# One PSUM ring for scores and transposed weights, and a third bank kept for the matmuls of the MLP, in a hybrid attention layer on one core

## The chip, the cores and the metric

The kernel runs on one core of one Trainium2 chip. The metric is the device time of one launch in microseconds, as the median of several runs. A profile of one execution comes with it: what each engine did and when, and what ended each stretch in which it was idle.

## What is computed

One step of a streaming encoder layer over 2048 prompt tokens and 32 sample tokens, with 1024 channels, all in fp32. The part of the reference that matters here is the long-range ("A") attention, with two softmax maps per head:

```python
def diff_core(q, k, v, bias, mask, lam):
    s = jnp.einsum('bqhmd,bkhmd->bhmqk', q, k).astype(jnp.float32) * (HEAD_DIM ** -0.5) + bias[:, None]
    s = jnp.where(mask, s, NEG)
    p = jax.nn.softmax(s, axis=-1)
    w = p[:, :, 0] - lam * p[:, :, 1]
    return jnp.einsum('bhqk,bkhe->bqhe', w.astype(v.dtype), v)
```

There are 4 such heads, and 8 heads of a short-range ("B") attention that sees the 64-token chunk and the 8 chunks before it. Both are fed by one input projection. Their outputs are normed, concatenated and projected (`w_out`), and added to the input. A squared-ReLU MLP with 4096 hidden channels, a gate (`w_ple_gate`, `w_ple_proj`) and a last norm follow.

## The kernel before

**Arithmetic.** Every fp32 operand of a matmul is split into a high and a low fp32r part. A product is three matmuls (`mm3`, lines 212 to 218): high by high, high by low, low by high. Line numbers 216, 217 and 218 therefore stand for the matmuls of every projection; the tile's name tells which: `ops` output projection, `ups` and `dps` the MLP's two halves, `gps` and `pps` the gate.

**Blocks.** Tokens come in four blocks of 512 (the last one with the 32 sample tokens). The A attention works on pairs of 128-query tiles, 256 queries, numbered j = 0 to 7; j = 8 stands for the sample. `JA0` (pairs 0 to 3) runs early; `JA1 = [(4, 5), (6, 7, 8)]` is the second long-range part. For each list of `JA1` the loop runs over the 4 heads, and in each head over the pairs of the list: 8 pairs, then 12, of which 4 are samples.

**One pair** (`attn_a_pair`, from line 597 on). For each of its two query tiles and each of the two maps, up to four score tiles `s` of 128 x 512 are computed (line 639, two matmuls each) and moved by VectorE to `e`, with the row maximum taken on the way (line 646; line 648 where the bias `ba` is added, which happens in the last block only). ScalarE takes the exponential of the whole row (654), and ScalarE and VectorE combine the two maps into weights (659, 660). `e` has two buffers for each map, one for each query tile, so a pair can't empty its first scores before the weights of the pair before it have been transposed. Then, for each 512 keys and each query tile, TensorE transposes the weights four to a tile `tpp` (698), ScalarE and VectorE read it as `pH` (705) and `pL` (706), and three matmuls per 128 keys add into `o` (712 to 714), which ScalarE moves to `os` (716). The bias tile `ba` of a head has one buffer, `q` has two.

**PSUM.** There are eight banks of 128 x 512 fp32. Up to and through the projection of the last two blocks they are: `mm` 2 and `mmx` 1 (projections, MLP; a `Rings` object hands them out as mm, mm, mmx in turn), `pss` 2 (scores), `pst` 2 (transposes), `pso` 1. Before the second long-range part the kernel closes `mmx`, so that output projection and MLP have the two banks of `mm`, and opens its bank as `psy`: scores then take turns in three banks (s, s, y) and transposes in their own two. After the MLP of blocks 0 and 1 all attention pools are closed and their six banks become `md`, for the gate and what follows.

**What sets the order.** Nothing of the order on an engine is written by hand here. A scheduler that simulates the program fixes it at build time: each engine takes what is ready, and of several ready instructions the one that stands first in the program. The second long-range part stands in the program before the output projections and the MLP of blocks 0 and 1. In the order of execution they are mixed: whenever the attention has nothing ready, matmuls of the MLP are put in. Each engine then takes its instructions strictly in that order, and waits at semaphores where the chip is later than the simulation. Two rules of the scheduler matter: the tiles of one pool and tag get their buffers in the order in which the program asks for them, a later one never ahead of an earlier one; different pools know nothing of each other. All loads and stores go through the one queue of SP (line 157).

The lines in question, the second long-range part and what follows it, are these:

Of the kernel before, what the change touches and what calls it, by code (L numbers as in the profile page):

```python
# [18 lines left out]
PSUM = bass.MemoryType.PSUM  # L19
# [64 lines left out]
def drain(gen):  # L84
    for _ in gen:
        pass
# [57 lines left out]
class Kern:  # L144
# [1296 lines left out]
    def run(self):  # L1441
        tc, nc, a = self.tc, self.nc, self.a
        with ExitStack() as top:

            def opened(stack, name, bufs, space=None, side="left"):
                kw = {} if space is None else {"space": space}
                return stack.enter_context(
                    tc.tile_pool(name=name, bufs=bufs, side=side, reuse_waits="tile", **kw)
                )
# [7 lines left out]
            opened(top, "edge", 1, side="right").tile([P, 24], F32, name="edge")  # L1457
            mm = opened(top, "mm", MM, PSUM)
            mmx = ExitStack()
            mz = mm  # L1460
            mm = Rings((mz, "mm"), (mz, "mm"), (opened(mmx, "mmx", 1, PSUM), "mm"))
            tp = mm
            psx = ExitStack()
            ps_s = opened(psx, "pss", 4 - MM, PSUM, "right")
            ps_t = opened(psx, "pst", 2, PSUM, "right")
            ps_o = opened(psx, "pso", 1, PSUM, "right")
# [39 lines left out]
            with ExitStack() as x:  # L1506
                pool = opened(x, "a0", 1, side="right")
# [42 lines left out]
            drain(self.oload(0, wq, actq, oa))  # L1550
            wqx.close()
            bx.close()
            mmx.close()
            mm = mz
            ps_y = opened(psx, "psy", 1, PSUM, "right")
            sy = Rings((ps_s, "s"), (ps_s, "s"), (ps_y, "s"))
            with ExitStack() as x:
                pool = opened(x, "a1", 1, side="right")
                for js in JA1:
                    self.attn_a(js, pool, sy, ps_t, ps_o)  # L1560
            self.nt = 4
            wk = opened(sq_, "wk", 1)
            fk = opened(sq_, "fk", 1)
# [23 lines left out]
            for b in HALVES[0]:  # L1587
# [10 lines left out]
                if b == 0:  # L1598
                    self.dma(self.hS[:, :, 512 * b : 512 * b + 512], h)
            psx.close()  # L1600
            md = opened(top, "md", 8 - MM, PSUM, "right")
            drain(self.gate(1, h, uq, actq, md))
            drain(self.final(1, h, uq, fk, mm))
# [101 lines left out]
```

## Time and profile before

| what | value |
|---|---|
| median of 3 runs | 3122.03 us (3116.57 to 3123.8) |
| the profiled execution's own time | 3116.1 us |
| its span, first to last instruction | 3114.0 us |
| mean granted TensorE clock | 0.986 |
| first and last MLP matmuls of blocks 0 and 1 (`ups` to `dps`) | 992.8 to 2035.7 us |
| first and last `s` matmul of the second long-range part | 1229.9 to 1888.3 us |
| its last transpose | 1920.9 us |

How to read it: PE is TensorE's matmuls and PEld its weight loads, which run beside them. DVE is VectorE, ACT ScalarE, POOL GpSimd, SP the engine that issues the DMAs. A line of a group or of the time order names the line of code, the operation, and the tile that is written and those that are read (`e<-s`). What stands after an arrow in brackets is the idle time of the engine just before the instruction, and whose work ended it. "PEclk", the granted clock, is a share of the full clock. A matmul's duration includes its tail in the pipeline: 512-column matmuls that last 0.39 us start every 0.23 us.

### The profile page before, as it was taken

Reading aid. Unit: us, or ns where it says so; the run is one execution under the profiler, and the core shown is the slowest. Engines: PE = TensorE matmul, PEld = TensorE weight load, DVE = VectorE, ACT = ScalarE, POOL = GpSimd, SP = SyncE. Lnnn points to the kernel's source line nnn. Section 1 sums busy time; section 2 is a strip of 40 time slices with the busy share of each in tenths; the row PEclk is TensorE's granted clock in tenths of the full one; section 3 lists DMA queues with packets and bytes.
Section 4 is the critical chain, followed back from the end, with each engine's and each line's share of the span. In section 5 each row is a group of like instructions: output and inputs, shape, how many; then the busy total and the mean of one; then the engine's idle time right before and its main releaser. Section 6 shows DMA issues by size and latency. Waiting matters only on the chain. (4 is left out here: it accounts for less than half of the span.)

```text
span 3114.0 us, 51781 instructions
## 1 busy us (share of the span) xinstructions
PE 2992.9 (96%) x17801; PEld 2639.7 (85%) x17801; DVE 1815.1 (58%) x4404; ACT 1779.4 (57%) x3446; POOL 1859.1 (60%) x2512
## 2 busy tenths in 40 slices
PE   8998988999999999999999999999899999999998
PEld 7787877999877887788788888779788887999998
DVE  5256574654466554566655654425667884576663
ACT  6256665765666774566655645454655545554545
POOL 2456745423445543665645556677878888767674
PEclk9999999999999999999999999999999999999999
DMA  9797866976788555565665443538434446333231
GB/s 285 261 263 226 243 199 211 269 225 197 213 248 268 154 148 139 151 172 147 192 173 146 126 122 108 162 98 261 154 116 136 139 159 223 117 109 102 89 117 57
DMA packets 523278, 539.19 MB, mean 173 GB/s; under 512 B 38748, under 2 KB 401568, under 8 KB 523016
## 3 DMA queue, kind: packets, MB, share of 16 engines
q1 hardware_dynamic: 523016, 535.89, 57.3%
q8 instruction: 141, 2.31, 0.3%
q14 instruction: 121, 0.99, 0.1%
HBM read 421.97 MB, written 117.75 MB: 173 GB/s over the span
## 5 line engine op out<-in xcount | busy, mean ns | idle before, releaser
L176 POOL TENSOR_TENSOR wl<-wr,wh 128x256 fp32r<-128x256 f32 x648 | 482.3, 776 | 322.6 <-ACT wh L181 271.2
L181 ACT ACTIVATE piece<-wr 128x512 fp32r<-128x512 f32 x406 | 245.8, 625 | 269.2 <-PE ups L217 116.0
L176 POOL TENSOR_TENSOR piece<-wr,piece 128x256 fp32r<-128x256 f32 x404 | 326.5, 834 | 101.9 <-ACT piece L181 80.7
L181 ACT ACTIVATE wh<-wr 128x1024 fp32r<-128x1024 f32 x228 | 240.5, 1056 | 224.7 <-PE ups L217 56.8
L166 POOL TENSOR_TENSOR wl<-wr,wh 128x256 fp32r<-128x256 f32 x264 | 197.2, 777 | 166.9 <-ACT wh L181 162.0
L216 PE MATMUL dps<-uh,piece 128*128 128x272 f32 (+1 forms) x768 | 246.4, 324 | 7.2 <-ACT piece L181 2.9
L166 POOL TENSOR_TENSOR piece<-wr,piece 128x256 fp32r<-128x256 f32 x280 | 234.4, 868 | 27.8 <-ACT piece L181 24.9
L1158 DVE TENSOR_TENSOR h<-h,dps 128x512 f32<-128x512 f32 x256 | 174.2, 683 | 130.1 <-PE dps L218 128.6
L218 PE MATMUL dps<-uh,piece 128*128 128x272 f32 (+1 forms) x768 | 247.1, 324 | 1.3 <-POOL piece L166 1.1
L217 PE MATMUL dps<-ul,piece 128*128 128x272 f32 (+1 forms) x768 | 247.3, 323 | 0.2 <-DVE ul L187 0.2
L216 PE MATMUL ups<-cs,piece 128*128 128x256 f32 (+1 forms) x864 | 245.7, 285 | 1.6 <-DVE r L1217 1.6
L217 PE MATMUL ups<-cs,piece 128*128 128x256 f32 (+1 forms) x864 | 245.7, 285 | 0.0
L218 PE MATMUL ups<-cs,piece 128*128 128x256 f32 (+1 forms) x864 | 245.5, 284 | 0.0
L216 PE MATMUL qps<-aH,wh 128*128 128x512 f32 (+1 forms) x640 | 228.6, 357 | 1.2 <-DVE ql L477 0.9
L217 PE MATMUL qps<-aL,wh 128*128 128x512 f32 (+1 forms) x640 | 227.2, 355 | 0.0
L218 PE MATMUL qps<-aH,wl 128*128 128x512 f32 (+1 forms) x640 | 227.0, 355 | 0.0
L1206 DVE TENSOR_TENSOR h<-h,dps 128x272 f32<-128x272 f32 (+1 forms) x384 | 189.1, 514 | 51.9 <-PE dps L218 51.1
L216 PE MATMUL dps<-uh,wh 128*128 128x512 f32 x512 | 211.6, 413 | 7.0 <-ACT relu L1123 4.4
L654 ACT ACTIVATE e<-e,nm 128x128 f32<-128x128 f32 (+16 forms) x136 | 157.1, 1156 | 97.4 <-DVE nm L652 96.9
L217 PE MATMUL dps<-ul,wh 128*128 128x512 f32 x512 | 203.5, 397 | 0.0
L218 PE MATMUL dps<-uh,wl 128*128 128x512 f32 x512 | 203.1, 397 | 0.0
L216 PE MATMUL ups<-cH,wh 128*128 128x512 f32 x512 | 202.0, 395 | 0.5 <-ACT relu L1123 0.5
(310 smaller groups left out, 9370.5 us busy)
## 6 DMA issues: line engine op xcount, KB each, us to landing
wr<-w_up SPq DMA_DIRECT2D x128, 512.0 KB, 3.9
wr<-w_down SPq DMA_DIRECT2D x128, 512.0 KB, 3.8
wr<-w_in SPq DMA_DIRECT2D x74, 512.0 KB, 5.5
q<-qS SPq DMA_DIRECT2D x128, 256.0 KB, 5.6
v<-vSa SPq DMA_DIRECT2D x64, 512.0 KB, 3.6
ka<-kS SPq DMA_DIRECT2D x32, 512.0 KB, 8.0
wr<-w_out SPq DMA_DIRECT2D x32, 512.0 KB, 5.0
wr<-w_ple_gate SPq DMA_DIRECT2D x32, 512.0 KB, 4.2
```

The source lines that it names most:

```text
L166: nc.gpsimd.tensor_tensor(out[:, sl], a[:, sl], b[:, sl], op=op)
L176: nc.gpsimd.tensor_tensor(out[:, sl], a[:, sl], b[:, sl], op=op)
L181: nc.scalar.activation(hi, raw, AF.Copy)
L216: nc.tensor.matmul(ps, lh, rh, start=start and i == 0, stop=False)
L217: nc.tensor.matmul(ps, lh, rl, start=False, stop=False)
L218: nc.tensor.matmul(ps, ll, rh, start=False, stop=stop and i == n - 1)
L654: nc.scalar.activation(row, row, AF.Exp, bias=nmx, accum_out=z[:nr, m : m + 1])
L1158: nc.vector.tensor_tensor(hv, hv, ps, op=ALU.add)
L1206: nc.vector.tensor_tensor(hv, hv, ps, op=ALU.add)
```

## The change

```diff
-            mz = mm
+            mm0 = mz = mm
             mm = Rings((mz, "mm"), (mz, "mm"), (opened(mmx, "mmx", 1, PSUM), "mm"))
...
             wqx.close()
             bx.close()
-            mmx.close()
-            mm = mz
-            ps_y = opened(psx, "psy", 1, PSUM, "right")
-            sy = Rings((ps_s, "s"), (ps_s, "s"), (ps_y, "s"))
+            mz = mm
+            sy = Rings((ps_s, "s"), (ps_t, "tp"), (ps_s, "s"), (ps_t, "tp"))
             with ExitStack() as x:
                 pool = opened(x, "a1", 1, side="right")
                 for js in JA1:
-                    self.attn_a(js, pool, sy, ps_t, ps_o)
+                    self.attn_a(js, pool, sy, sy, ps_o)
...
             psx.close()
+            mmx.close()
+            mm = mm0
             md = opened(top, "md", 8 - MM, PSUM, "right")
```

`mmx` stays open until the MLP of blocks 0 and 1 is done, so the output projections of blocks 0 and 1, their norms and the MLP take turns in three banks (mm, mm, mmx). `psy` isn't opened. Scores and transposed weights of the second long-range part both ask the one ring `sy`, which gives them the two banks of `pss` and the two of `pst` alternately, in the order of the program: for one pair up to 16 score tiles, then up to 8 transposed tiles, then the next pair's scores. After the MLP `mmx` is closed too, so `md` again has six banks, one of which is now the one of `mmx` in place of that of `psy`; the ring `mm` becomes the two-bank pool again for the last norm.

Nothing else is changed. The short-range attention keeps `pss` and `pst` as two separate pools.

## The prediction

> **What bounds the kernel now.** I read the page first, then the busy table by stage, then what TensorE waited for between 790 and 2045 us, and last the instructions in order of time around each of the longer waits.
>
> ```profile
> span 3114.0 us, 51781 instructions
> PE 2992.9 (96%) x17801; PEld 2639.7 (85%) x17801; DVE 1815.1 (58%) x4404; ACT 1779.4 (57%) x3446; POOL 1859.1 (60%) x2512
> ```
>
> TensorE is busy for 96% of the span and nothing else passes 60%. Its work isn't changed here (the same matmuls in another order), so the change can only move TensorE's idle time and its clock. The stages, whose columns are window, length, then busy time of PE, PEld, DVE, ACT, POOL, granted clock, DMA share and GB/s:
>
> ```profile
> 1040.00:1220.00 180.00, 180.00 (x915) 150.37 (x914) 98.63 (x341) 118.77 (x246) 80.60 (x123) 1.00 0.48 135
> 1220.00:1942.00 722.00, 701.70 (x3608) 591.55 (x3607) 432.50 (x1029) 419.95 (x650) 416.10 (x577) 0.99 0.54 151
> 1942.00:2036.00 94.00, 92.88 (x402) 74.67 (x401) 40.11 (x55) 38.99 (x54) 68.23 (x93) 1.00 0.51 162
> ```
>
> The second long-range part (JA1) runs from 1220 to 1942, always mixed with MLP matmuls, and there TensorE is idle 722 - 701.7 = 20.3 us. That is nearly all that can be won. Who made it wait, in the wider window (total, times, longest):
>
> ```profile
> PE s L639 <- DMA q<-qS: 9.7, 4, 3.8
> PE dps L216 <- ACT relu L1123: 4.4, 2, 4.0
> PE dps L216 <- DVE h L1158: 2.1, 4, 0.8
> PE tpp L698 <- DVE e L660: 2.0, 1, 2.0
> PE s L639 <- DVE e L646: 1.4, 1, 1.4
> PE css L1085 <- ACT relu L1123: 0.5, 1, 0.5
> PE ups L216 <- ACT relu L1123: 0.5, 1, 0.5
> ```
>
> The reader is to see that only some of these are waits for a bank: the MLP's (dps, css, ups behind relu or h: 4.4 + 2.1 + 0.5 + 0.5 = 7.5 us) and one of scores behind e (1.4). The largest, scores behind the load of q, is no bank wait.
>
> **Part 1: scores can no longer run ahead (a gain).** Three of the four q waits stand at the same place, the step from one head to the next within JA1's second list (6, 7, 8):
>
> ```profile
> 1596.18 1.05 PE L639 MATMUL s<-ka,q 128*128 128x512 f32 x4 [0.71 <-DMA q<-qS]
> 1690.24 1.17 PE L639 MATMUL s<-ka,q 128*128 128x512 f32 x4 [2.71 <-DMA q<-qS]
> 1793.48 1.58 PE L639 MATMUL s<-ka,q 128*128 128x512 f32 x4 [3.81 <-DMA q<-qS]
> 1813.85 0.93 PE L698 MATMUL tpp<-ident,e 128*128 128x128 f32 x7
> 1814.81 0.31 DVE L648 CUSTOM_DVE_ANT_0 e<-s,ba 32x160 f32<-32x160 f32 x1 [5.98 <-PE tpp L698]
> 1820.36 0.69 DVE L646 TENSOR_SCALAR_CACHE_REDUCE e<-s 128x512 f32<-128x512 f32 x1 [1.35 <-PE tpp L698]
> 1822.55 0.27 PE L698 MATMUL tpp<-ident,e 32*128 32x32 f32 x2
> ```
>
> Each time four matmuls (two score tiles of the next head) stop TensorE until q has landed. At 1793.48 they stop it for 3.81 us, though VectorE empties them only at 1820.36, 27 us later, because e is still being transposed. They run so early because scores have a ring of their own with a bank free. In the new ring a tile takes its place in the program's order, so these two stand behind the transposes of the head's last full pair (to 1813.85) and the sample's scores; q has then been there for 20 us. The waits go: 0.71 + 2.71 + 3.81 = 7.2 us. The clock after two of them goes too:
>
> ```profile
> 1580.00:1600.00 20.00, 19.29 (x90) 15.55 (x89) 12.95 (x29) 14.67 (x20) 13.53 (x18) 1.00 0.87 205
> 1680.00:1700.00 20.00, 17.29 (x77) 13.74 (x76) 12.01 (x25) 10.65 (x15) 12.18 (x16) 0.91 0.93 219
> 1780.00:1800.00 20.00, 16.20 (x73) 13.11 (x72) 12.72 (x27) 10.83 (x17) 12.49 (x15) 0.91 0.75 185
> ```
>
> Two windows at 0.91 lose 2 x 20 x 0.09 = 3.6 us. Together **-10.8 us**. [...]
>
> What is late next? The pair's first evacuations, which now wait for fresh matmuls in place of ready tiles: a score tile is two matmuls, 0.63 us in the rows above, so about 1 us per pair for the attention. TensorE fills that with MLP work, as long as there is some:
>
> ```profile
> L716 ACT ACTIVATE os<-o x20: 176/384/386, 1273.7 to 1929.1; 128x256 f32<-128x256 f32 x16, 128x32 f32<-128x32 f32 x4
> L1158 DVE TENSOR_TENSOR h<-h,dps x256: 659/686/691, 1035.1 to 2036.1; 128x512 f32<-128x512 f32 x128
> ```
>
> The attention's 20 pairs leave o by 1929 and JA1's window closes at 1942; the MLP has work until 2036. That is 94 us of room, 94 / 20 = 4.7 us per pair. So I cost the longer chain at nothing; without that cover it would be 20 us at 1 us per pair. Queues: score and transpose instructions change places on PE; the later release of the sample's q delays the next q load on SP's queue, and weight loads stand behind it. I cost that at nothing too, because the load isn't needed until a whole pair later; its bound is under the rivals.
>
> **Part 2: a third bank for MLP and projections (a small gain).** The longest bank wait:
>
> ```profile
> 1294.98 1.06 ACT L181 ACTIVATE wh<-wr 128x1024 fp32r<-128x1024 f32 x1 [6.41 <-DMA wr<-w_up]
> 1295.94 0.58 ACT L1123 ACTIVATE relu<-ups 128x512 f32<-128x512 f32 x1
> 1290.15 0.39 PE L216 MATMUL dps<-uh,wh 128*128 128x512 f32 x1
> 1291.53 1.03 PE L698 MATMUL tpp<-ident,e 128*128 128x128 f32 x8
> 1296.57 0.80 PE L216 MATMUL dps<-uh,wh 128*128 128x512 f32 x1 [4.01 <-ACT relu L1123]
> ```
>
> ScalarE sat behind a late load of w_up for 6.41 us with relu queued behind it, so the bank of ups stayed full and dps had none. A third bank lets one more dps tile through: six matmuls, 1290.15 to 1291.53, **-1.4 us**; the tile after it would stop at the same relu. Bounds: 0, and all 4.01 us with the clock that followed:
>
> ```profile
> 1280.00:1300.00 20.00, 15.99 (x73) 13.17 (x72) 7.26 (x14) 12.37 (x21) 13.05 (x20) 0.89 0.84 206
> 1300.00:1320.00 20.00, 20.00 (x110) 17.38 (x110) 15.09 (x40) 10.83 (x17) 11.11 (x16) 0.94 0.46 150
> ```
>
> (0.11 + 0.06) x 20 = 3.4, so 7.4 us. The other bank waits, 2.1 + 0.4 + 0.5 + 0.5 = 3.5 us, are all shorter than the 1.4 us of one dps tile, so I let them go: **-3.5 us**, bound 0.
>
> [...]
>
> **Part 3: scores and transposes in four banks together, where they had three and two (a loss).** The trace has no shared ring. The nearest row is JA0, the same code with two and two banks, between 150 and 480 us:
>
> ```profile
> PE s L639 <- DVE e L646: 3.2, 3, 1.4
> ```
>
> JA0 has 16 pairs, so 3.2 / 16 = 0.2 us a pair; 20 pairs make **+4.0 us**. The upper bound takes the longest such wait in every pair, 20 x 1.4 = 28 us. The lower is -1.4: the one such wait of JA1 itself could go, since for runs of scores alone four banks are more than three.
>
> Part 4: the third bank is closed only after the MLP, so one of md's six banks comes free with the last dps tiles and not long before. Between nothing and one dps tile, 1.4 us; the gate has five other banks: 0.
>
> **Sum**: -10.8 - 1.4 - 3.5 + 4.0 = -11.7 us. The profiled execution took 3116.1 us (span 3114.0), which gives 3104.4. The median of the runs shown is 3122.0, 5.9 above the profiled one, so **3110 us**. A measurement of this kernel tells about 0.2%, 6.2 us, from no change.
>
> **The rivals.**
>
> *The loads stay late* (no change). For: the w_up row above shows the same lateness elsewhere, and the bias tile of a head, single-buffered, is fetched only after the sample's evacuation, which now comes later:
>
> ```profile
> L331 POOL MEMSET ba<- x8: 144/144/158, 1221.5 to 1819.0; 64x64 f32 x8
>   DMA ba<-dba: 24.5, 7
> ```
>
> GpSimd waited 24.5 us in 7 fetches, 3.5 each; VectorE's queue could wait as long, and dps evacuations behind it. Against: the scores that need the bias are a pair's last block. Then part 1 brings nothing: -4.9 + 4.0 = -0.9, **3121 us**.
>
> *The third bank brings nothing*: -10.8 + 4.0 = -6.8, **3115 us**. For: relu sits behind a load. Against: the short waits.
>
> *All waits go*: -10.8 - 7.4 - 3.5 - 1.4 = -23.1, **3099 us**.
>
> *The ring couples the two* (slower). TensorE takes instructions strictly in its order, and a score tile now needs a bank that ScalarE and VectorE must both have read (pH, then pL), just after the last transposes of a pair. Where they run late, all MLP matmuls queued behind wait as well. At 1.4 us a pair: -15.7 + 28 = +12.3, **3134 us**; it decides from (15.7 + 6.2) / 20 = 1.1 us a pair. For: before, the early scores needed nothing just then. Against: JA0's 0.2 us.
>
> *The attention outlasts the MLP* (slower). If each pair is longer by VectorE's longest wait for a transpose, 5.98 us above, 20 x 6 - 94 = 26 us stick out: -15.7 + 26 = +10, **3132 us**, from 4.7 us a pair on. Against: with four banks the transposes of a pair's first tile no longer stand behind those of its second.
>
> That the change doesn't do what it says (banks not gained) I rule out: 2 + 1 + 2 + 2 + 1 is eight.
>
> **How the numbers follow.** Forecast 0.40; third bank nothing 0.12; all waits 0.06; loads stay late 0.18; ring couples 0.17; attention outlasts 0.07. Faster by over 0.2% (below 3115.8): 0.40 + 0.06 + two thirds of 0.12 = 0.54. Within: 0.04 + 0.18 = 0.22. Slower: 0.24. The forecast's own range is 3099 to 3115; with the slow rivals' prices the range is 3097 to 3136.
>
> **What would show it.** Right: no wait of s for q at the heads of list (6, 7, 8); no score tile that lies over 10 us before its evacuation; dps waits for relu shorter; the attention's last os before 2036. Wrong: s or tpp waiting for e, pH or pL 20 times; waits of VectorE for ba; PE idle after 1942; or new waits for wr, since a changed order shifts every load on SP.

## The result, and the profile after

The changed kernel takes **3112.55 us** (median of 12 runs, 3106.55 to 3118.47) against 3122.72 us (12 runs, 3114.97 to 3132.71) for the kernel before: a ratio of 0.9966, 95% interval 0.9954 to 0.9978, or about 10 us less. The forecast was 3110. The experiments below show that the sum came out nearly right while its terms did not all do so.

The head of the page of the changed kernel:

```profile
span 3108.6 us, 51779 instructions
PE 2987.4 (96%) x17801; PEld 2634.6 (85%) x17801; DVE 1825.9 (59%) x4404; ACT 1780.4 (57%) x3446; POOL 1858.2 (60%) x2512
```

Against before (span 3114.0, PE busy 2992.9) TensorE is busy 5.5 us less, and idle as long as before (3108.6 - 2987.4 = 121.2, before 121.1). The number of matmuls is the same (17801), and the mean granted clock is 0.989 against 0.986 before; so the reading is that in these two executions it is the clock that shows in the total. By stage it looks different. The busy table of the changed kernel, then that of the kernel before, for 754 us within the second long-range part and for 1090 us around it:

```profile
1262.00:2016.00 754.00, 744.01 (x3821) 627.98 (x3820) 460.84 (x1061) 439.58 (x682) 446.86 (x624) 1.00 0.54 152
1000.00:2090.00 1090.00, 1068.17 (x5392) 896.01 (x5391) 624.79 (x1547) 648.93 (x1080) 621.30 (x877) 0.99 0.52 148
```

```profile
1262.00:2016.00 754.00, 737.11 (x3754) 619.54 (x3753) 441.69 (x1022) 432.17 (x665) 449.64 (x622) 0.99 0.52 150
1000.00:2090.00 1090.00, 1064.04 (x5344) 889.66 (x5342) 609.24 (x1522) 639.30 (x1059) 619.33 (x867) 0.99 0.52 147
```

In the inner window the idle time falls from 754 - 737.11 = 16.9 to 10.0 us, and the clock rounds to 1.00; in the wider one only from 26.0 to 21.8. So about 7 us of idle time are won in the stage, and part of that is lost behind it. What TensorE waited for between 790 and 2045 us, after the change:

```profile
PE ups L216 <- ACT cH L181: 3.9, 2, 2.0
...
PE dps L216 <- ACT relu L1123: 3.6, 2, 3.0
...
PE s L639 <- DVE e L646: 2.1, 2, 1.6
...
PE s L639 <- DMA q<-qS: 1.8, 1, 1.8
```

The waits of s for q went from 9.7 us in 4 to 1.8 in 1, and that one is the start of the stage, not a step between heads. The waits of dps for h (2.1) and of tpp for e (2.0) are gone too. The wait of dps for relu is still there, and ups now waits for cH. One of the steps from head to head, in order of time:

```profile
1673.53 1.03 PE L698 MATMUL tpp<-ident,e 128*128 128x128 f32 x8
...
1677.42 0.31 PE L639 MATMUL s<-ks,q 128*32 128x160 f32 x2
...
1680.35 0.66 PE L639 MATMUL s<-ka,q 128*128 128x512 f32 x2
...
1681.05 0.69 DVE L646 TENSOR_SCALAR_CACHE_REDUCE e<-s 128x512 f32<-128x512 f32 x1
...
1688.30 0.27 PE L698 MATMUL tpp<-ident,e 32*128 32x32 f32 x2
```

The next head's first score tile (1680.35) now stands behind the transposes and the sample's scores, waits for nothing, and is emptied 0.7 us later, where at one such step before it lay for 27 us. It does not stand behind every transpose: those of the sample's weights come at 1688.30. The ring hands out banks in the order of the program, but a score tile that has its bank can still be computed before a transpose that waits for its weights. In the traces of the changed kernel and of the ring alone (below), one to four score tiles of the next pair come before the last one to three transposed tiles of a pair, at every step within list (4, 5) and at every step between heads in list (6, 7, 8). The clock in the same two windows as before:

```profile
1680.00:1700.00 20.00, 19.48 (x101) 16.07 (x100) 9.45 (x36) 7.57 (x17) 11.71 (x20) 1.00 0.60 161
1780.00:1800.00 20.00, 18.67 (x95) 15.36 (x94) 9.11 (x32) 7.15 (x17) 11.32 (x19) 1.00 0.62 175
```

The longest bank wait of the MLP has moved to 1302.75 us and has the same pattern, a weight load that ScalarE waits for with relu queued behind it:

```profile
1301.14 1.06 ACT L181 ACTIVATE wh<-wr 128x1024 fp32r<-128x1024 f32 x1 [8.14 <-DMA wr<-w_down]
...
1305.15 0.57 ACT L1123 ACTIVATE relu<-ups 128x512 f32<-128x512 f32 x1
1305.78 0.50 PE L216 MATMUL dps<-uh,wh 128*128 128x512 f32 x1 [3.03 <-ACT relu L1123]
```

Two things were not foreseen. The attention moved back: the short-range attention, which the change doesn't touch, transposes its last tile 56 us later (first the kernel before, then the changed one), and the second long-range part follows:

```profile
L842 PE MATMUL tpb<-ident,eb x576: 188/272/478, 525.9 to 1205.5; 128*128 128x128 f32 x187, 32*128 32x32 f32 x3, 32*32 32x32 f32 x2
```

```profile
L842 PE MATMUL tpb<-ident,eb x576: 188/272/473, 525.4 to 1261.7; 128*128 128x128 f32 x187, 32*128 32x32 f32 x3, 32*32 32x32 f32 x2
L716 ACT ACTIVATE os<-o x20: 176/384/386, 1340.2 to 1994.6; 128x256 f32<-128x256 f32 x16, 128x32 f32<-128x32 f32 x4
L216 PE MATMUL dps<-uh,wh x79: 387/393/483, 1900.0 to 2014.9; 128*128 128x512 f32 x79
```

The last os is at 1994.6 in place of 1929.1, and the last dps at 2015 in place of 2035: 20 us of room are left, where the prediction counted on 94 (by the same two rows it was 106 before). The likely reason is that a third bank lets more MLP matmuls be ready, and that they take TensorE's time from the attention: between 1000 and 1210 us, 345 matmuls of ups and 129 of sb (the short-range scores) run in the changed kernel, against 327 and 140 with the ring alone (below).

And after the MLP there is a new loss. The 74 us from 2016 on, before and after:

```profile
2016.00:2090.00 74.00, 72.38 (x323) 59.16 (x321) 24.32 (x35) 36.32 (x56) 48.02 (x66) 1.00 0.32 96
```

```profile
2016.00:2090.00 74.00, 65.79 (x280) 53.16 (x281) 27.11 (x38) 38.72 (x63) 48.31 (x66) 0.95 0.47 141
```

Idle time 8.2 us in place of 1.6, and a clock of 0.95 (74 x 0.05 = 3.7 us). The longest wait there:

```profile
2046.42 0.63 ACT L181 ACTIVATE piece<-wr 128x512 fp32r<-128x512 f32 x1 [4.21 <-DMA wr<-w_out]
...
2047.13 1.41 POOL L176 TENSOR_TENSOR piece<-wr,piece 128x256 fp32r<-128x256 f32 x2 [4.05 <-ACT piece L181]
2048.50 1.40 POOL L166 TENSOR_TENSOR h<-h,sig 128x256 f32<-128x256 f32 x2
2049.27 0.47 PE L1392 MATMUL yp<-ident,h 128*128 128x128 f32 x1 [3.75 <-POOL h L166]
```

A load of w_out was late by 4.21 us; GpSimd's split of it stood ahead of its addition to h, and TensorE stood behind that. No bank is in it.

### The profile page after: what moved, and what is told of

Read it like the earlier page. It is cut to its first block, busy times and chain, and to the rows that moved or that the text cites. A ratio compares the mean times of both kernels' runs of the same rounds, so it can differ in the third digit from the quotient of the medians.

```text
span 3108.6 us, 51779 instructions
## 1 busy us (share of the span) xinstructions
PE 2987.4 (96%) x17801; PEld 2634.6 (85%) x17801; DVE 1825.9 (59%) x4404; ACT 1780.4 (57%) x3446; POOL 1858.2 (60%) x2512
## 5 line engine op out<-in xcount | busy, mean ns | idle before, releaser
L217 PE MATMUL ups<-cL,wh 128*128 128x512 f32 x512 | 203.4, 397 | 1.2 <-POOL cL L166 1.2
L218 PE MATMUL ups<-cH,wl 128*128 128x512 f32 x512 | 203.3, 397 | 0.0
```

Of the source, the lines that this page charges most:

```text
L217: nc.tensor.matmul(ps, lh, rl, start=False, stop=False)
L218: nc.tensor.matmul(ps, ll, rh, start=False, stop=stop and i == n - 1)
```

## The experiments

Each kernel ran in five rounds beside the kernel before; a ratio is to the runs of before on the same chip (medians there 3122.89 for the first four, 3123.76 for the next four, 3117.93 for the last). Theory 1 is the prediction's: the run-ahead of the scores cost the time, and its end is worth 10.8 us by itself. Theory 2 came up after the first four: what counts is which banks are within reach of the transposes.

### The ring alone, and the third bank alone

The ring alone (`mmx` closed as before, one bank idle):

```diff
             bx.close()
-            mz = mm
+            mmx.close()
+            mm = mz
             sy = Rings((ps_s, "s"), (ps_t, "tp"), (ps_s, "s"), (ps_t, "tp"))
...
             psx.close()
-            mmx.close()
-            mm = mm0
```

> The shared ring of four alone; output projection and MLP keep two banks, and one bank lies idle. Against the kernel before (3122.7 us). Theory 1 (the scores' run-ahead cost the time: waits for q 7.2 us and clock 3.6 us, the ring costs 4.0): 3116 us, and no wait of s for q at the heads of list (6, 7, 8). Theory 2 (the third bank makes the gain): no gain here, 3122 to 3127 us. Theory 3 (any change of the order moves the waits about, neither part matters as such): anywhere within 3117 to 3128, with waits at other places.

Measured: 3111.18 us, ratio 0.9967 (0.9954 to 0.9979). That is the whole of the change's gain. The waits for q went as in theory 1 (1.7 us, once). The idle time between 1000 and 2090 us is 18.8 us, and its pairs of list (4, 5) are shorter than before, not longer. The ring alone has this row, and below it are the moments in which `o` is moved out, in the ring alone and then in the kernel before:

```profile
1000.00:2090.00 1090.00, 1071.18 (x5393) 895.19 (x5391) 612.58 (x1531) 646.83 (x1071) 628.47 (x885) 1.00 0.52 150
```

```profile
L716 ACT ACTIVATE os<-o x8: 367/384/386, 1269.6 to 1506.0; 128x256 f32<-128x256 f32 x8
```

```profile
L716 ACT ACTIVATE os<-o x8: 359/384/386, 1273.7 to 1520.6; 128x256 f32<-128x256 f32 x8
```

(1506.0 - 1269.6) / 7 = 33.8 us a pair against 35.3. In the changed kernel it is 37.2 (1340.2 to 1600.9): the third bank makes a pair 3.4 us longer.

The third bank alone (`mmx` open, no shared ring):

```diff
-            sy = Rings((ps_s, "s"), (ps_t, "tp"), (ps_s, "s"), (ps_t, "tp"))
...
-                    self.attn_a(js, pool, sy, sy, ps_o)
+                    self.attn_a(js, pool, ps_s, ps_t, ps_o)
```

> The third bank for output projection and MLP alone; scores keep two banks of their own and transposes two, so scores can still run ahead by two tiles. Against the kernel before (3122.7 us). Theory 1: 3.5 to 4.9 us less from bank waits, the waits for q at the heads of list (6, 7, 8) stay at 5 to 10 us: 3118 us. Theory 2: all of the gain, 3112 us. Rival: scores with two banks in place of three wait for e more often, 0.2 us in each of 20 pairs: 3122 us.

Measured: 3184.23 us, ratio 1.0200 (1.0187 to 1.0213), beyond all three expectations. A pair takes 46.6 us, the attention outlasts the MLP (last os at 2090.3, last dps at 1960.9), and then nothing covers its chain:

```profile
L716 ACT ACTIVATE os<-o x8: 364/372/386, 1354.2 to 1680.6; 128x256 f32<-128x256 f32 x8
```

```profile
2016.00:2090.00 74.00, 50.96 (x246) 38.49 (x246) 43.99 (x123) 37.98 (x64) 14.24 (x22) 0.80 0.20 61
```

```profile
PE tpp L698 <- DVE e L660: 20.6, 7, 5.2
```

This is the prediction's rival "the attention outlasts the MLP", in a kernel that has only half of the change.

Which half of that kernel does it, the two banks for scores or the third for the MLP? The same with `mmx` closed and two banks for the MLP:

```diff
             bx.close()
+            mmx.close()
+            mm = mz
```

> Scores two banks of their own, transposes two, output projection and MLP two, one bank idle: the kernel with the third bank alone (3184 us) without the third bank. Theory A (two banks for scores are too few, whatever the MLP has): pairs of list (4, 5) at 42 to 47 us, the attention outlasts the MLP, 3160 to 3185 us. Theory B (the third bank lets MLP matmuls crowd the attention out of TensorE): pairs at 35 to 38 us as before, 3120 to 3128 us.

Measured: 3138.48 us, ratio 1.0043 (1.0028 to 1.0057). Pairs take 41.1 us. Two and two banks apart cost some 13 us, and the third bank on top of that 1.0200 - 1.0043 = 0.0157, another 49 us. Both theories had a part of it, and theory B the larger.

### Is the run-ahead the cause?

The kernel before, with its banks as they are; only the order on TensorE is changed, so that the scores of a pair come behind the last transpose of the pair before. That is stricter than the shared ring, which lets one to four score tiles run before the last transposes:

```diff
-                            nc.tensor.matmul(
+                            with self.tc.issue_after(self.tail) if self.tail else ExitStack(): nc.tensor.matmul(
                                 s[:, x0:x1], q[:, m, hl, P * qi : P * qi + nr],
...
-                    nc.tensor.transpose(tp[:kn, x, :nr], w[:nr, P * i : P * i + kn], self.ident[:nr, :nr])
+                    tail = nc.tensor.transpose(tp[:kn, x, :nr], w[:nr, P * i : P * i + kn], self.ident[:nr, :nr])
...
-        os_ = pool.tile([P, 256], F32, tag="os", bufs=2, name="os")[:, :nq]
+        os_ = pool.tile([P, 256], F32, tag="os", bufs=2, name="os")[:, :nq]; self.tail = None if self.small else tail.ins
```

> The kernel before with its three score banks and two transpose banks apart; only the order on TensorE is changed: in the second long-range part the scores of a pair are put behind the last transpose of the pair before it, as the shared ring puts them. Theory 1 (the scores' run-ahead cost the time): the waits of s for q at the heads of list (6, 7, 8) go, 3111 to 3113 us. Theory 2 (it is the banks: four of one ring, all of them open to whichever of the two is next, make a pair shorter): the waits for q go but come back as other waits, pairs of list (4, 5) stay at 35 us, 3119 to 3124 us.

Measured: 3126.20 us, ratio 1.0007 (0.9997 to 1.0018): no gain. The waits for q did go (one of 2.0 us is left, the start). In their place pairs take 42.2 us, the attention ends with the MLP (last os at 2022.3, last dps at 2029.9), and its tail lies open:

```profile
L716 ACT ACTIVATE os<-o x8: 362/384/388, 1278.1 to 1573.4; 128x256 f32<-128x256 f32 x8
```

```profile
PE ss L723 <- DVE sh L183: 5.2, 1, 5.2
PE tpp L698 <- DVE e L660: 5.2, 4, 3.2
```

So theory 1 falls as it stood: the end of the waits for q is not by itself worth 10.8 us. The ring of four, with one bank fewer, takes 1.0007 - 0.9967 = 0.0040, 12.5 us, less. This is not the worth of the ring at the same order, because the order differs too. At one step between heads in this kernel, the next head's scores all stand behind the sample's transposes, where in the changed kernel's trace six score matmuls stand before them (two of these in the rows above):

```profile
1792.78 0.27 PE L698 MATMUL tpp<-ident,e 32*128 32x32 f32 x2
1792.98 1.53 PE L639 MATMUL s<-ka,q 128*128 128x512 f32 x6
```

To leave the pairs alone, the next kernel puts that order only at the three steps between heads, where the waits for q were, of list (6, 7, 8):

```diff
-        os_ = pool.tile([P, 256], F32, tag="os", bufs=2, name="os")[:, :nq]; self.tail = None if self.small else tail.ins
+        os_ = pool.tile([P, 256], F32, tag="os", bufs=2, name="os")[:, :nq]; self.tail = tail.ins if samp else None
```

> The kernel before with one order changed on TensorE: only at the three steps from one head to the next of list (6, 7, 8) the next head's scores are put behind the sample's last transpose; banks as before (scores three, transposes two, MLP two). Theory 1 in its narrow form (the three waits for q cost 7.2 us and 3.6 us of clock, and taking them away is worth that as long as the attention ends before the MLP): 3112 to 3114 us, last os before 2016. Theory 2 (what counts is that transposes reach more banks; a wait that is taken away at the heads comes back elsewhere): 3119 to 3126 us.

Measured: 3129.18 us, ratio 1.0032 (1.0020 to 1.0045): slower, and neither theory expected that. The attention ends in time (1954.5), and no wait for q is left but the start's. At the same steps between heads there is now this, at 1610 and again, with 4.49, at 1717 us:

```profile
1613.58 1.06 ACT L181 ACTIVATE wh<-wr 128x1024 fp32r<-128x1024 f32 x1 [7.60 <-DMA wr<-w_up]
1614.55 0.58 ACT L1123 ACTIVATE relu<-ups 128x512 f32<-128x512 f32 x1
...
1615.18 0.50 PE L216 MATMUL dps<-uh,wh 128*128 128x512 f32 x1 [4.57 <-ACT relu L1123]
```

```profile
PE dps L216 <- ACT relu L1123: 14.7, 4, 4.6
```

A head's `ka`, `ks`, `q` and the weights all come through one queue at that moment: the two loads of w_up ahead of that row are issued from 1602.86 on, behind eight of `q`, `ka` and `ks` from 1595.70 on. Here, with q out of the way, the two-bank MLP stops behind w_up instead, and the wait for q reads as one face of a late stretch of loads. It need not go so: in the kernel with the order changed at every pair, dps waits 0.3 us behind relu between 1262 and 2016 us, and with the ring alone 4.6 us, both with two banks for the MLP.

### More banks for the transposes, or for both

The bank `psy` given to the transposes in place of the scores (two and three), in the kernel before:

```diff
-            sy = Rings((ps_s, "s"), (ps_s, "s"), (ps_y, "s"))
+            ty = Rings((ps_t, "tp"), (ps_t, "tp"), (ps_y, "tp"))
...
-                    self.attn_a(js, pool, sy, ps_t, ps_o)
+                    self.attn_a(js, pool, ps_s, ty, ps_o)
```

> The kernel before with the bank psy given to the transposes in place of the scores: scores two, transposes three, MLP two. Theory 1: one score tile fewer runs ahead, the waits for q stay in part: 3116 to 3122 us. Theory 2 (more banks within reach of the transposes make a pair shorter): pairs of list (4, 5) at 34 us, 3112 to 3116 us. Rival (scores need the third bank): 3125 to 3160 us.

Measured: 3112.68 us, ratio 0.9955 (0.9942 to 0.9969), as much as the change. But its pairs of list (4, 5) take 38.6 us, not 34, so the reason given for theory 2 (shorter pairs) is not the one. Its last os is at 1983.0, 44 us before its last dps (2027.0), and its waits for q are 2.9 us in 2. What it shares with the ring is that the waits for q are short and that the attention still ends before the MLP. So the gain needs no shared ring. With two banks for the scores, a third for the transposes is worth 1.0043 - 0.9955 = 0.0088, 27 us.

The ring alone with the idle bank taken in as `psy`, five in turn:

```diff
+            sy = Rings((ps_s, "s"), (ps_t, "tp"), (ps_y, "s"), (ps_s, "s"), (ps_t, "tp"))
```

> The shared ring of four alone (3111 us) with the idle fifth bank taken into the ring (s, tp, y, s, tp); output projection and MLP have two. Theory 1: nothing more to gain, the scores already stand in order: 3110 to 3112 us. Theory 2: pairs of list (4, 5) below 33.8 us, 3105 to 3110 us. Rival (a longer ring lets scores and transposes run ahead again): waits for q or v come back, 3113 to 3118 us.

Measured: 3125.52 us, ratio 1.0006 (0.9994 to 1.0017): the gain of the ring of four is lost. The attention is the quickest of all (last os at 1852.7), and that is no use:

```profile
PE dps L216 <- DVE h L1158: 11.3, 9, 3.1
PE o L712 <- DMA v<-vSa: 6.7, 2, 5.8
```

The reading that fits these rows is that an attention which already ends before the MLP wins nothing by more speed, crowds VectorE, which also empties the MLP's two banks, and asks for v sooner than it comes. No run tests it. The waits for q are as short here (2.5 us, once) as in the ring of four.

### A third buffer for q (inconclusive)

In the kernel before, and then in the changed one, with the same edit:

```diff
-        q = pool.tile([P, 2, 2, 256], F32R, tag="q", bufs=2, name="q")
+        q = pool.tile([P, 2, 2, 256], F32R, tag="q", bufs=2 if self.small else 3, name="q")
```

> The kernel before with three buffers for q in the second long-range part, so that q of the next head can be loaded one pair earlier; scores still run ahead in their three banks, and nothing else is changed. Theory 1: the three waits for q at the heads of list (6, 7, 8) and the clock behind them go, 10.8 us: 3112 us, as much as with the shared ring. Rival (loads are late because the SP queue and the DMA engines are behind, not for want of a buffer): the waits stay, 3122 us. Rival (the wait moves on to the bias tile or to wr): 3118 to 3122 us.

> The changed kernel with three buffers for q in the second long-range part. Theory 1: its scores have no early place any more, so an earlier q is worth only the one wait left, at most 1.8 us: 3111 to 3113 us. Rival (q still sets the pace of the pairs): 3105 to 3109 us. Theory 3 (each change of the order moves the waits about): some 5 us either way.

Measured: 3461.63 us (1.1085, 1.1070 to 1.1099) and 3437.86 us (1.1012, 1.0997 to 1.1026). The MLP no longer mixes with the attention: in the first of them its first ups is at 1637.0, after the last os (1555.9).

It may be that the larger pool leaves no room for the MLP's tiles beside it; that was not tried. For the question of q these two say nothing. The mixing that they lack may be worth as much as 339 us in the kernel before and 327 us in the changed one.

### Better versions

The ring alone, with the first long-range part on the ring too, and then the short-range attention as well:

```diff
-            self.small = True
+            self.small = True; sy = Rings((ps_s, "s"), (ps_t, "tp"), (ps_s, "s"), (ps_t, "tp"))
...
-                    self.attn_a(js, pool, ps_s, ps_t, ps_o)
+                    self.attn_a(js, pool, sy, sy, ps_o)
...
-                self.attn_b(js, bp, ps_s, ps_t, ps_o)
+                self.attn_b(js, bp, sy, sy, ps_o)
```

> The shared ring of four alone (3111 us) with the first long-range part on the same ring too (it had two and two banks apart). Theory 2 (transposes that reach four banks shorten a pair and leave fewer waits): the stage between 150 and 480 us has waits of s for e (3.2) and of o for pH, pL (6.0) to lose: 3103 to 3108 us. Rival (there the attention shares TensorE with little other work, and e, not the banks, sets the pace): 3109 to 3113 us. Rival (fewer score tiles run ahead, with no MLP to fill in): 3114 to 3120 us.

> As the one before, and the short-range attention on the shared ring too. Theory 2: its waits of tpb and sb (5.1 and 7.7 us) shrink, 3098 to 3107 us. Rival (its scores run ahead by four tiles on purpose, and the ring puts them behind transposes): the waits of sb and tpb grow, 3115 to 3135 us.

Measured: 3111.20 us, ratio 0.9980 (0.9969 to 0.9990), no gain over the ring alone; and 3099.79 us, ratio 0.9930 (0.9917 to 0.9942), a gain. In the second the waits of sb for stb between 520 and 1220 us are these, against 9.0 us with the ring alone:

```profile
PE sb L820 <- DVE stb L823: 2.5, 5, 1.0
```

The changed kernel, with two banks for the output projections and the third only from the MLP on:

```diff
-            mz = mm
+            mz = mm3 = mm; mz = mm = mm0
...
-            hq = opened(sq_, "hq", 1)
+            hq = opened(sq_, "hq", 1); mm = mm3
```

> The changed kernel with two banks for the output projections of blocks 0 and 1 and the third only for their MLP. Theory C (the third bank brings nothing, because the matmuls it lets through only take TensorE's time from the attention, and the pieces they need come no sooner): as the ring alone and as the changed kernel, 3110 to 3114 us, with the short-range attention ending at 1209 us again and the pairs of list (4, 5) at 36 to 38 us. Rival (it is worth the 4.9 us of the forecast once the short-range attention isn't held up): 3105 to 3108 us.

Measured: 3095.68 us, ratio 0.9925 (0.9911 to 0.9938), the lowest ratio of all, level with the ring everywhere within the intervals, and beyond both expectations. The short-range attention ends at 1240.6, pairs take 37.5 us, the last os is at 1976.8. And the loss behind the MLP is not there:

```profile
2016.00:2090.00 74.00, 72.24 (x321) 58.77 (x320) 20.97 (x32) 39.92 (x63) 53.66 (x76) 1.00 0.39 114
```

Against the changed kernel's row that is 6.5 us of idle time and 3.7 us of clock. The third bank does pay here, by 0.9967 - 0.9925 = 0.0042, 13 us against the ring alone.

How it pays is not shown. The forecast's reason was that it lets matmuls by while relu sits behind a late load. These are ScalarE's waits for weights between 1262 and 2016 us, in the changed kernel, in the one with two banks and the order changed at the heads, and in the one with two and two banks apart and two for the MLP:

```profile
ACT wh L181 <- DMA wr<-w_down: 20.9, 4, 8.1
ACT wh L181 <- DMA wr<-w_up: 19.7, 6, 4.8
```

```profile
ACT wh L181 <- DMA wr<-w_up: 21.2, 4, 7.6
...
ACT wh L181 <- DMA wr<-w_down: 5.7, 1, 5.7
```

```profile
ACT wh L181 <- DMA wr<-w_down: 16.7, 2, 9.6
ACT wh L181 <- DMA wr<-w_up: 7.7, 2, 6.8
```

40.6 us of late weights made dps wait 3.0 us behind relu with three banks, and 26.9 us made it wait 14.7 with two. That looks like cover by the bank, but 24.4 us in the third kernel, also with two banks, made dps wait for relu not at all. In the kernel with the third bank from the MLP on it is 4.3 us for 28.3. So the sum of the late loads does not tell how long dps waits, with two banks or with three.

## Why the prediction was right and wrong

**What bounds the kernel** was read rightly: TensorE's idle time and clock in this stage. Between 1000 and 2090 us TensorE idles 26.0 us before, 16.4 to 25.2 in the six kernels that are quicker (the changed one among them), and 30.6 to 56.6 in the five that are level or slower, the two with a third buffer for q apart. The prediction's list of waits leaves out those of sb for stb (6.8 us) and of ops for oact (4.5 us), which are the second and third longest of that window before. The first can be won: in the kernel with the ring everywhere the waits of sb for stb are short (2.5 us), and it is one of the two quickest.

**Part 1 (-10.8)** is right in every row that it named: the waits for q at the heads are gone, scores are emptied at once (0.7 us later at the step shown), and the clock is 1.00. Whether it is right as a term by itself stays open. The two kernels that end the waits by the order alone are at +0.0007 and +0.0032, but their order is stricter than the ring's, so they charge more than part 1 did. In the first the pairs pay, with 42.2 - 35.3 = 6.9 us each, above the 4.7 us of room that the prediction gave; in the second dps stops behind w_up. Of all the kernels, the six that are quicker than before wait at most 2.9 us for q in the second long-range part, but so do three that are level or slower (2.0 to 2.5 us). The end of these waits goes with every gain and is not enough for one. The step "What is late next?" was answered with about 1 us more per pair. The ring alone makes a pair 1.5 us shorter, and the whole change makes it 1.9 us longer, of which the third bank accounts for 3.4.

**Part 3 (+4.0)** charged a loss that isn't there: waits of s for e are 2.1 us in two places with the change, and with the ring alone there are none in the second long-range part, where the prediction had 0.2 us in each pair. The row from the first long-range part was a poor neighbour: there it was two and two banks apart, which here costs 13 us. Parts 1 and 3 together were forecast at -6.8; the ring alone measured -10.3 (-6.6 to -14.4). That fits part 1 as costed with part 3 at nothing, and it fits a smaller part 1 with some gain by the banks; no run tells the two apart.

**Part 2 (-4.9)** is the term that is most clearly off: it came out at about nothing, since the change and the ring alone have nearly the same ratio (0.9966 and 0.9967). Their intervals leave some 5 us either way, so a small gain is not excluded. The rival "the third bank brings nothing" describes the net, though its time, 3115, was off by part 3. That net is not what the third bank gave elsewhere: -13 us when it was kept for the MLP, and +49 us beside two and two banks apart. What the forecast left out is that the bank also shifts the attention back by 65 us, and that 10 us are lost again at the gate, behind a load of w_out that was 4.21 us late. The first was costed nowhere; the second is the sign "new waits for wr" that the prediction listed.

That the total came so near is luck in part: by the medians the ring gave 3.5 us more than parts 1 and 3, and the third bank almost 5 us less than part 2.

**Part 4 (0)** is right as far as the bank goes: the kernel with the third bank for the MLP alone frees it as late, and has no such loss.

**The rivals.** The ring didn't couple the two. The attention didn't outlast the MLP, but 20 us of room were left, and half the change alone has none. "The loads stay late" was at work in part, though not as forecast: not through `ba`, but through w_down, w_up and w_out.

What stays open: each arrangement is another order fixed at build time, and one kernel of each ran. The bank counts are one cause; where a load happens to fall is another, and the 13 us of the last kernel were not split between them. A profile is one execution (that of the last kernel took 3104.2 us, 8.5 above its median, and only 3.5 below the profiled one of the ring alone), so stage differences of a few us between two profiles are a hint and no more.

## What to carry to other kernels

A wait at the head of an engine's queue named here the transfer that came last, not the time to be won: before it is costed, ask what the engine would stop at next if that transfer had been in time. Here that was in one kernel the weights that come through the same queue (dps 14.7 us behind relu, ratio 1.0032), in another the attention's own chain (pairs of 42.2 us, ratio 1.0007). Work that filled in for a latency-bound chain also competed with it here: the third bank for the filler went with pairs 3.4 us longer, the attention's room was 106 us before the change and 20 after, and with that bank beside two and two banks apart the attention ended 129 us after the MLP (ratio 1.0200). So the room belongs in the sum. And where two uses of a memory take turns, one ring of four served better here (0.9967) than three and two apart (the kernel before); two and three apart served as well (0.9955), and a fifth bank in the ring took the gain away (1.0006).

## What the runs showed of the hardware

In these two stretches the longer idle time is not the one with the lower clock behind it. In the changed kernel 1.78 us of idle time are followed by 5 us at a granted clock of 0.66, a loss of 5 x 0.34 = 1.7 us; in the last kernel 2.29 us of idle time are followed by 5 us at 1.00:

```profile
1285.00:1290.00 5.00, 3.22 (x17) 2.53 (x16) 1.08 (x4) 1.86 (x3) 1.42 (x2) 1.00 1.09 270
1290.00:1295.00 5.00, 5.00 (x16) 3.93 (x16) 1.56 (x7) 1.35 (x2) 0.00 (x0) 0.66 1.07 222
```

```profile
1340.00:1345.00 5.00, 2.71 (x17) 2.21 (x16) 3.43 (x6) 1.84 (x3) 4.92 (x8) 1.00 0.33 79
1345.00:1350.00 5.00, 5.00 (x39) 4.80 (x38) 2.48 (x8) 4.54 (x12) 4.29 (x7) 1.00 0.85 254
```
